# Retention's products as sums of two-part products, short tails stacked into full-height operands, key parts kept in the sample states' buffers

## The chip, the cores and the metric

The kernel runs on one core of a Trainium2 chip. The metric is the device time of one execution in microseconds (us), and lower is better. A core has a matrix engine (TensorE, PE in the profile, with its weight loads as PEld), a vector engine (VectorE, DVE), a scalar engine (ScalarE, ACT), GpSimd (POOL) and a queue engine (SyncE, SP) which here issues almost all DMA transfers.

## The reference

One layer of a decoder trunk for 256 prompt tokens, 16 learned meta tokens ahead of them, and 8 sample tokens, which makes T = 280 columns (TL = 264 without the meta tokens). All of it is in fp32.

```python
x <- LN1(alpha*x + 0.5*SwiGLU_1(x))      # 2048 -> 5504 -> 2048
x <- LN2(alpha*x + Mixer(x))             # x @ w_in (2048 -> 10*2048), retention + HGRN2, gates, w_out
x <- LN3(alpha*x + 0.5*SwiGLU_2(x))
```

The mixer has two branches. Retention has 8 heads with 256 key and 256 value features and a fixed decay per head: the outputs are (q k^T * D) v, normalised over the head's features by mean and variance, and the prompt's state is the sum over tokens of decayed k times v. HGRN2 has 16 heads of 128 features with a learned forget gate, and its prompt state is likewise a sum over tokens. The sample tokens each update a state of their own (`state_ret`, `state_hgrn`), which is read, updated, written back and multiplied with the sample's query.

## The kernel before

Activations lie with features on the 128 partitions and tokens along the free dimension, as 16 chunks of 128 features. Each dense product is made of parts: an fp32 operand is split into a rounded part `hi` (type fp32r, made by ScalarE) and a rest `lo` (made by VectorE), and a 128x128 block of weights takes three matmuls, whi*xhi, whi*xlo and wlo*xhi (`dense`, lines 196 to 198). Weights stream in units of 8 blocks: SP loads `raw`, ScalarE makes `whi` (L170), VectorE makes `wlo` (L171), with three buffers for each (`stream`). A matmul with plain fp32 operands appears in the profile as two instructions.

The order on TensorE is written out by hand; the other engines' instructions are put in order by the compiler's planner, by priority and by due times that it models. Engines and the SP queue work strictly in the order they were given.

In the mixer, the loop `for u in range(HR)` projects six groups of two output chunks (f, q_h, i_h, q_r, k_r, v_r) for head pair u and then four gate groups for u-1. A group walks over the 16 chunks of x, and after each chunk, that is after 6 dense matmuls, `pump()` counts one step for every running thread. A thread is a Python generator, `mix_hg` for two HGRN2 heads or `mix_ret` for one retention head; `yield n` means that its next piece of TensorE work is put in n steps later. `start(gen, 3)` starts a thread three steps after the group that completes its inputs. `evacuate` for the gates of u needs the threads of u to be done.

`mix_ret` does, in order: transposes of v (L780) and k (L786) through a PSUM bank, decayed keys `kt` (L788), scores `psc` (L799) and their decay (`mul(scr...)`, with the table `dtab`), the prompt state `psr` (L811) for two halves c, the sample states in two halves e (loads L825, scaling on ScalarE L826, update on VectorE L829, store L832, product `pqr` L838), the outputs `por` (L852, and L854 for the samples), the mean `pm` (L861) and the variance. `mix_hg` transposes v (L637), makes the within-chunk attention over seven levels, and then for each of its two heads h transposes the keys (L717), copies them out (`kth` L718, and the 16 meta rows `ktm` L719), updates the sample states (L726, L727), and after `yield 6` makes the state products `pst` (L735 with the 16-row operands, L736, L737).

The tokens are 16 + 256: as blocks of 128 rows they leave a 16-row tail (the last tokens in `mix_ret`, the meta tokens in `mix_hg`), so that one matmul of each state sum and each output has operands 16 rows high.

`tmp(name, ...)` gives a buffer: either one of its own in the pool `mp` or, for the names in `rows`, one of the row tiles d0 to d15, ls1 and so on, which other names use at other times. `smr` has three buffers, for the retention sample states. `y` (the mixer's output in parts) has hi and lo of chunk c apart by 288 values for c below `Y_SPACED` and by 264 from there on.

Of the kernel before, what the change touches and what calls it, by code (L numbers as in the profile page):

```python
# [18 lines left out]
P = 128  # L19
# [4 lines left out]
NMETA, SEQ, NS = 16, 256, 8  # L24
LP = NMETA + SEQ
T = LP + NS
TL = T - NMETA
# [6 lines left out]

WT = U * P + 64
XT = 576
Y_SPACED = 12
XL = {T: 296, T + 2: 284, TL: 288, TL + 2: 288}
HL = {T: 296, TL: 288}
SG = {T: 296, TL: TL}  # L40
# [12 lines left out]
SCORES = ((0, 0, SEQ, P), (SEQ, P - NMETA, 2 * P - P + NMETA, P), (2 * SEQ - P + NMETA, SEQ - NMETA, NMETA, LP - 2 * P))  # L53
NSC = SCORES[2][0] + SCORES[2][2]
# [58 lines left out]
def trunk(ctx: ExitStack, tc: tile.TileContext, A, O):  # L113
    nc = tc.nc
    cst = ctx.enter_context(tc.tile_pool(name="cst", bufs=1))
# [24 lines left out]
    olb = cst.tile([P, KC], F32, tag="olb", name="olb")  # L140
    dec = cst.tile([P, 3, HR], F32, tag="dec", name="dec")
    sel = cst.tile([P, NS], F32, tag="sel", name="sel")
    msk = cst.tile([P, MASKED + 1, 2 * P], U8, tag="msk", name="msk")
    lnb = cst.tile([P, 2, 2, KC], F32R, tag="lnb", name="lnb")
    nc.vector.memset(ones, 1.0)
# [56 lines left out]
    def split(hi, lo, x):  # L202
        nc.scalar.copy(hi, x)
        nc.vector.tensor_tensor(out=lo, in0=x, in1=hi.bitcast(F32), op=ALU.subtract)

    def sums(out, hilo, part=slice(None)):

        for i, x in enumerate(hilo):
            nc.tensor.matmul(out, ones_r, x[:, part], start=i == 0, stop=i == 1)

    def mul(out, a, b):
        nc.vector.tensor_tensor(out=out, in0=a, in1=b, op=ALU.mult)

    def add(out, a, b):
        nc.vector.tensor_tensor(out=out, in0=a, in1=b, op=ALU.add)
# [253 lines left out]
    nc.sync.dma_start(ident, A["ident"])  # L469
    nc.sync.dma_start(dec, A["dec"])  # L470
    nc.sync.dma_start(sel, A["sel"])

    norm1 = ffn(1, up1, A["w_dn1"], 1)


    with tc.tile_pool(name="yp", bufs=1) as yp:
        yh, yl = [None] * KC, [None] * KC
        with tc.tile_pool(name="mp", bufs=1) as mp:

            rows = {n: (r if isinstance(r, list) else [r]) for n, r in {  # L480
# [3 lines left out]
            }.items()}  # L484
# [22 lines left out]
            st = {}  # L507
# [4 lines left out]
            qdr = tmp("qdr", (P, 2, NS * 32))  # L512
            nc.gpsimd.memset(qdh, 0.0)
            nc.gpsimd.memset(qdr, 0.0)
            threads = []

            def pump(_=None):
# [8 lines left out]
            def start(gen, wait):  # L526
                threads.append([gen, wait])
# [16 lines left out]
            def evacuate(n, c0, c1, o0, o1):  # L544
# [16 lines left out]
                elif n == "i_h":  # L561
                    v = tmp("v", (P, 2, T))
                    nc.scalar.copy(v[:, 0, :], o0)
                    nc.scalar.copy(v[:, 1, :], o1)
                    start(mix_hg(c0 // 2, st["f"], st["k"], st["q"], v), 3)
                elif n in ("q_r", "k_r"):
                    sc, w, x0 = (1.0, TL, NMETA) if n == "q_r" else (KSC, T, 0)
                    r = tmp(n, (P, 2, w))
# [36 lines left out]
            NB2 = LP - 2 * P  # L605
            BLOCKS = ((0, P), (P, P), (2 * P, T - 2 * P))

            def rows_out(src, width, tag):

                scr = drp.tile([NS, width], F32, tag=tag + "d", name=tag + "d")  # L610
                nc.sync.dma_start(scr, src)
                return scr

            def mix_hg(u, f, k, q, v):
# [9 lines left out]
                for i in range(3):  # L624
# [6 lines left out]
                vt = tmp("vth", (P, 2, 4, P))  # L631
                vrow = []
                for h in range(2):

                    pt = mx_bank("pt")
                    for b, (t0, n) in enumerate(((NMETA, P), (NMETA + P, P), (0, NMETA), (T - NMETA, NMETA))):
                        nc.tensor.transpose(pt[:n, b * P : (b + 1) * P], v[:, h, t0 : t0 + n], ident)  # L637
                    nc.scalar.copy(vt[:, h, 0:2, :], pt[:, : 2 * P].rearrange("p (b f) -> p b f", b=2))
                    nc.scalar.copy(vt[:NMETA, h, 2:4, :], pt[:NMETA, 2 * P :].rearrange("p (b f) -> p b f", b=2))
                    vrow.append(rows_out(vt[8:16, h, 3, :], P, f"vh{h}"))  # L640
                    yield 1
                yield 5
                pd = mx_bank("pd")
# [67 lines left out]
                on_h[u] = on  # L711
                for h in range(2):
                    kt = tmp("kth", (P, 2, P))
                    ktm = tmp("ktm", (P, P))
# [4 lines left out]
                    nc.scalar.copy(ktm[:NMETA, :], pt[:NMETA, 2 * P : 3 * P])  # L719

                    vb = tmp("vbh", (P, NS, P))
                    nc.sync.dma_start(vb, vrow[h].partition_broadcast(P))
# [5 lines left out]
                            out=sm[:, b, :], in0=vb[:, b, :], scalar=k[:, h, LP + b : LP + b + 1], in1=sm[:, b, :],  # L728
                            op0=ALU.mult, op1=ALU.add)
                    nc.sync.dma_start(O["sgs"][2 * u + h], sm)  # L730
                    yield 6

                    S = tmp("Sh", (P, 3, P))
                    pst = mx_bank("pst")
                    nc.tensor.matmul(pst[:, 0:P], ktm[:NMETA, :], vt[:NMETA, h, 2, :], start=True, stop=True)  # L735
                    nc.tensor.matmul(pst[:, P : 2 * P], kt[:, 0, :], vt[:, h, 0, :], start=True, stop=True)  # L736
                    nc.tensor.matmul(pst[:, 2 * P : 3 * P], kt[:, 1, :], vt[:, h, 1, :], start=True, stop=True)  # L737
                    nc.scalar.copy(S[:, 0, :], pst[:, :P])
# [31 lines left out]
                done_h.add(u)  # L770

            def mix_ret(u, q, k, v):
                vt = tmp("vtr", (P, 3, 2, P))
                kt = tmp("ktr", (P, 3, 2, P))
                dt = tmp("dtab", (P, NSC))
                nc.sync.dma_start(dt, A["dtab"][u])
                for c in range(2):
                    pt = mx_bank("pt")
                    for b, (t0, n) in enumerate(BLOCKS):
                        nc.tensor.transpose(pt[:n, b * P : (b + 1) * P], v[:, c, t0 : t0 + n], ident)  # L780
                    nc.scalar.copy(vt[:, 0:2, c, :], pt[:, : 2 * P].rearrange("p (b f) -> p b f", b=2))
                    nc.scalar.copy(vt[: BLOCKS[2][1], 2, c, :], pt[: BLOCKS[2][1], 2 * P : 3 * P])
                    yield 1
                    pt = mx_bank("pt")
                    for b, (t0, n) in enumerate(BLOCKS):
                        nc.tensor.transpose(pt[:n, b * P : (b + 1) * P], k[:, c, t0 : t0 + n], ident)  # L786
                    for b, (t0, n) in enumerate(BLOCKS):
                        nc.vector.tensor_scalar(  # L788
                            out=kt[:n, b, c, :], in0=pt[:n, b * P : (b + 1) * P], scalar1=dec[:n, b, u : u + 1],
                            scalar2=None, op0=ALU.mult)  # L790
                    yield 2
                nc.vector.tensor_copy(qdr[:, :, 0 : NS * 32 : 33], q[:, :, SEQ:])
                vtf = vt.rearrange("p b c f -> p b (c f)")
                vrow = rows_out(vtf[16:24, 2, :], 256, "vr")
# [7 lines left out]
                scr = dt  # L802
                c2 = SCORES[2][0]
                mul(scr[:, :c2], psc[:, :c2], dt[:, :c2])
                mul(scr[:NB2, c2:], psc[:NB2, c2:NSC], dt[:NB2, c2:])
                yield 2

                for c in range(2):
                    pst = mx_bank("psr")
                    for b, nr in enumerate((P, P, NB2)):  # L810
                        nc.tensor.matmul(pst[:, :256], kt[:nr, b, c, :], vtf[:nr, b, :], start=b == 0, stop=b == 2)  # L811
                    so = tmp("sro", (P, 256))
                    nc.scalar.copy(so, pst[:, :256])
                    nc.sync.dma_start(O["srp"][u, c], so)
                    yield 2

                os = tmp("osr", (P, 256))
                for e in range(2):
# [23 lines left out]
                        nc.scalar.copy(os, pq[:, :256])  # L842
                    else:
                        add(os, os, pq[:, :256])
                yield 3

                on = tmp("on_r", (P, 2, TL), bufs=2)
                on_r[u] = on
                for c in range(2):
                    po = mx_bank("por")  # L850
                    for b, (col, l0, n, nk) in enumerate(SCORES):
                        nc.tensor.matmul(  # L852
                            po[:, l0 : l0 + n], vt[:nk, b, c, :], scr[:nk, col : col + n], start=b == 0, stop=b == 2)
                    nc.tensor.matmul(po[:, SEQ:TL], os[:, c * P : (c + 1) * P], sel, start=True, stop=True)  # L854
                    nc.scalar.copy(on[:, c, :], po[:, :TL])
                    yield 1
                sm_ = tmp("sqr", (P, TL))
                add(sm_, on[:, 0, :], on[:, 1, :])
                yield 6
                pm = mx_bank("pm")  # L860
                nc.tensor.matmul(pm[:, :TL], ones, sm_, start=True, stop=True)  # L861
# [147 lines left out]
```

## Time and profile before

| | |
|---|---|
| three timed runs | 2843.91, 2850.09, 2852.86 us; median 2850.09 us |
| the profiled execution | 2834.7 us, its span 2832.9 us |
| granted TensorE clock | 0.998 |
| PE busy, VectorE busy, ScalarE busy | 2806.4 us, 1687.5 us, 1329.4 us |
| moved by DMA | 536.27 MB, mean 189 GB/s |

The span is the time from the first to the last instruction of the profiled execution. PE's busy time counts matmuls that overlap in the pipeline, so the occupation of the engine by one matmul is read from the distance of its start to the next one's start, not from its duration.

### The profile page before, as it was taken

What the parts mean: (1) busy time and instruction counts of PE and PEld (TensorE: products, weight loads), DVE (VectorE), ACT (ScalarE), POOL (GpSimd) and SP (SyncE); (2) the same over time, 40 slices, a digit from 0 to 9 for tenths busy, and PEclk for the clock granted to TensorE, in tenths of its full rate; (3) what the DMA queues carried; (4) which work ended last, traced back from release to release, by engine and by line L of the source; (5) the groups of instructions that cost most, each with busy time, mean ns of one, the idle gap of its engine ahead of it and who ended that gap; (6) DMA issues with size and microseconds to landing.
All of it is one profiled execution on the core that took longest, in us unless ns stands there. A gap on an engine that the chain in (4) does not pass through costs nothing.

```text
span 2832.9 us, 54281 instructions
## 1 busy us (share of the span) xinstructions
PE 2806.4 (99%) x22704; PEld 2753.0 (97%) x22704; DVE 1687.5 (60%) x2677; ACT 1329.4 (47%) x1931; POOL 3.4 (0%) x38
## 2 busy tenths in 40 slices
PE   9999999999999999999999999999999999999999
PEld 9999999999989999999999999989999999999998
DVE  5444444555586766676767676766884444446444
ACT  4444443443364564646464555545554444444333
POOL 0000000000000000000000000000000000000000
PEclk9999999999999999999999999999999999999999
DMA  6555555555556565656565666655555555555554
GB/s 223 173 176 173 172 175 175 171 173 175 174 186 215 197 229 191 226 193 226 197 222 198 223 195 222 195 195 178 179 179 179 183 182 179 181 183 180 179 180 141
DMA packets 154438, 536.27 MB, mean 189 GB/s; under 512 B 17808, under 2 KB 25936, under 8 KB 154192
## 3 DMA queue, kind: packets, MB, share of 16 engines
q1 hardware_dynamic: 154048, 532.65, 57.7%
q8 instruction: 178, 2.92, 0.4%
q14 instruction: 68, 0.56, 0.1%
q10 hardware_dynamic: 144, 0.14, 0.0%
HBM read 502.12 MB, written 30.61 MB: 188 GB/s over the span
## 4 chain that ended last, share of the span: by engine, by line
PE 95%; ACT 2%; DMA 1%; DVE 1%; issue 0%; SPq 0%; ACTq 0%; DVEq 0%
PE up L197 12%; PE up L198 12%; PE up L196 12%; PE dn L197 6%; PE dn L198 6%; PE dn L196 6%; PE pj_g_r L196 1%; PE pj_v_r L196 1%; PE pj_k_r L196 1%; PE pj_k_r L197 1%; PE pj_v_r L197 1%; PE pj_k_r L198 1%; PE pj_v_r L198 1%; PE pj_g_h L196 1%; PE wo L196 1%; PE wo L197 1%
## 5 line engine op out<-in xcount | busy, mean ns | idle before, releaser
L171 DVE TENSOR_TENSOR wlo<-raw,whi 128x1024 fp32r<-128x1024 f32 (+1 forms) x869 | 1062.8, 1223 | 900.6 <-ACT whi L170 897.1
L170 ACT CAST whi<-raw 128x1024 fp32r<-128x1024 f32 (+1 forms) x869 | 909.9, 1047 | 1137.2 <-PE up L197 481.2
L198 PE MATMUL up<-x,wlo 128*128 128x280 f32 (+1 forms) x2688 | 774.8, 288 | 1.2 <-DVE wlo L171 1.2
L197 PE MATMUL up<-x,whi 128*128 128x280 f32 (+1 forms) x2688 | 773.6, 288 | 0.0
L196 PE MATMUL up<-x,whi 128*128 128x280 f32 (+1 forms) x2688 | 765.8, 285 | 1.4 <-ACT whi L170 1.4
L196 PEld LDWEIGHTS up<-x,whi 128*128 128x128 f32 x2688 | 506.8, 189 | 2.0 <-ACT whi L170 2.0
L198 PEld LDWEIGHTS up<-x,wlo 128*128 128x128 f32 x2688 | 505.2, 188 | 1.8 <-DVE wlo L171 1.7
L197 PEld LDWEIGHTS up<-x,whi 128*128 128x128 f32 x2688 | 505.3, 188 | 0.0
L198 PE MATMUL dn<-h,wlo 128*128 128x280 f32 (+1 forms) x1376 | 396.1, 288 | 0.0
L197 PE MATMUL dn<-h,whi 128*128 128x280 f32 (+1 forms) x1376 | 395.6, 288 | 0.0
L196 PE MATMUL dn<-h,whi 128*128 128x280 f32 (+1 forms) x1376 | 391.9, 285 | 0.0
L196 PEld LDWEIGHTS dn<-h,whi 128*128 128x128 f32 x1376 | 259.1, 188 | 0.1
L197 PEld LDWEIGHTS dn<-h,whi 128*128 128x128 f32 x1376 | 258.4, 188 | 0.1
L198 PEld LDWEIGHTS dn<-h,wlo 128*128 128x128 f32 x1376 | 258.2, 188 | 0.0
L196 PE MATMUL pj_g_r<-x,whi 128*128 128x264 f32 x256 | 81.4, 318 | 0.0
L197 PE MATMUL pj_i_h<-x,whi 128*128 128x280 f32 x256 | 74.9, 292 | 2.7 <-DVE x L364 2.7
L196 PE MATMUL pj_g_h<-x,whi 128*128 128x264 f32 x256 | 76.8, 300 | 0.0
L196 PE MATMUL pj_i_h<-x,whi 128*128 128x280 f32 x256 | 74.2, 290 | 1.4 <-ACT f L549 0.7
L196 PE MATMUL pj_v_r<-x,whi 128*128 128x280 f32 x256 | 75.1, 293 | 0.0
L196 PE MATMUL pj_k_r<-x,whi 128*128 128x280 f32 x256 | 75.1, 293 | 0.0
L197 PE MATMUL pj_k_r<-x,whi 128*128 128x280 f32 x256 | 74.5, 291 | 0.0
L197 PE MATMUL pj_v_r<-x,whi 128*128 128x280 f32 x256 | 74.5, 291 | 0.0
(337 smaller groups left out, 5151.9 us busy)
## 6 DMA issues: line engine op xcount, KB each, us to landing
raw<-in_w_up SPq DMA_DIRECT2D x343, 512.0 KB, 3.6
raw<-in_w_in SPq DMA_DIRECT2D x320, 512.0 KB, 3.6
raw<-in_w_dn SPq DMA_DIRECT2D x172, 512.0 KB, 3.5
smr<-in_sr SPq DMA_DIRECT2D x32, 512.0 KB, 5.9
out_srs<-smr SPq DMA_DIRECT2D x32, 512.0 KB, 3.7
raw<-in_w_out SPq DMA_DIRECT2D x32, 512.0 KB, 3.6
smh<-in_sg SPq DMA_DIRECT2D x16, 512.0 KB, 4.0
out_sgs<-smh SPq DMA_DIRECT2D x16, 512.0 KB, 6.1
```

The source lines that it names most:

```text
L170: nc.scalar.copy(hi[:, j0:j1, :], raw[:, j0:j1, :])
L171: nc.vector.tensor_tensor(out=lo[:, j0:j1, :], in0=raw[:, j0:j1, :], in1=hi[:, j0:j1, :].bitcast(F32), op=ALU.subtract)
L196: nc.tensor.matmul(o, wh, h, start=k == 0, stop=False)
L197: nc.tensor.matmul(o, wh, l, start=False, stop=False)
L198: nc.tensor.matmul(o, wl, h, start=False, stop=k == nk - 1)
```

## The change

It concerns the mixer's threads, the buffers they use, and one constant.

- In `mix_ret`, v, the decayed keys, the decayed scores, the sample outputs `os` and the sum under the mean are split into hi and lo parts, and `psr`, `por`, the sample columns and `pm` are made of fp32r products: three for an operand pair of which both are split, two for a split operand with an exact one (`sel_r`, `ones_r`).
- `stack` writes a 16-row operand into a 128-row tile that is zero elsewhere, hi at two of the rows 0, 32 and 64 and lo at the third. One operand has lo at 32 and the other at 64, so that one fp32r matmul over 128 rows gives the three part products. Five `stack` calls per retention head (v and k of two halves, the scores) and four per HGRN2 thread (v and k of two heads) use it. The tiles are zeroed once, at the mixer's start.
- The key parts are tiles of the tag `smr`, so the three sample buffers also hold the keys; `dtab` comes in two pieces in the row tiles of `rot`; the tail of v lies in the row tile of `osr`, the tail of k in that of `sro`.
- Waits in steps: `yield 6` becomes 9 ahead of `pst`, `yield 3` becomes 5 ahead of `por`; the second HGRN2 thread (u = 1) starts after 25 steps and not after 3.
- `Y_SPACED` goes from 12 to 0.

The diff below is cut. Left out are: the scores, which are decayed in two pieces (256 and 144 columns) that are each split into `sch` and `scl`, with their 16-row tail stacked into `ss3`; and `por`, which has three products for each of two blocks, one for the tail (`vs3` with `ss3`) and two for the sample columns (`orh` and `orl` with `sel_r`).

```diff
-Y_SPACED = 12
+Y_SPACED = 0
+PARTS = (0, 32, 64)
...
     sel = cst.tile([P, NS], F32, tag="sel", name="sel")
+    sel_r = cst.tile([P, NS], F32R, tag="sel_r", name="sel_r")
...
+            vs3, ks3 = tmp("vs3", (P, 2, P), dt=F32R), tmp("ks3", (P, 2, P), dt=F32R)
+            ss3 = tmp("ss3", (P, NMETA), dt=F32R)
+            vm3, km3 = tmp("vm3", (P, 2, P), dt=F32R), tmp("km3", (P, P), dt=F32R)
+            for t in (vs3[:, 0, :], vs3[:, 1, :], ks3[:, 0, :], ks3[:, 1, :], vm3[:, 0, :], vm3[:, 1, :], km3, ss3):
+                nc.scalar.copy(t, qdh[:, 0, : t.shape[-1]])
+            def stack(tile_of, src, lo_at):
+                hi_at = [at for at in PARTS if at != lo_at]
+                first, other, low = (tile_of(slice(at, at + NMETA)) for at in hi_at + [lo_at])
+                nc.scalar.copy(first, src)
+                nc.scalar.copy(other, src)
+                nc.vector.tensor_tensor(out=low, in0=src, in1=first.bitcast(F32), op=ALU.subtract)
...
-                    start(mix_hg(c0 // 2, st["f"], st["k"], st["q"], v), 3)
+                    start(mix_hg(c0 // 2, st["f"], st["k"], st["q"], v), 25 if c0 == 2 else 3)
...
-                    nc.scalar.copy(vt[:NMETA, h, 2:4, :], pt[:NMETA, 2 * P :].rearrange("p (b f) -> p b f", b=2))
+                    nc.scalar.copy(vt[:NMETA, h, 2, :], pt[:NMETA, 3 * P :])
+                    stack(lambda r: vm3[r, h, :], pt[:NMETA, 2 * P : 3 * P], 32)
...
-                    nc.scalar.copy(ktm[:NMETA, :], pt[:NMETA, 2 * P : 3 * P])
+                    stack(lambda r: km3[r, :], pt[:NMETA, 2 * P : 3 * P], 64)
...
-                    yield 6
+                    yield 9
-                    nc.tensor.matmul(pst[:, 0:P], ktm[:NMETA, :], vt[:NMETA, h, 2, :], start=True, stop=True)
+                    nc.tensor.matmul(pst[:, 0:P], km3, vm3[:, h, :], start=True, stop=True)
...
-                vt = tmp("vtr", (P, 3, 2, P))
-                kt = tmp("ktr", (P, 3, 2, P))
-                dt = tmp("dtab", (P, NSC))
+                vh, vl = tmp("vtr", (P, 2, 2, 2, P), dt=F32R).rearrange("p e b c f -> e p b c f")
+                kh, kl = tmp("ktr", (P, 2, 2, 2, P), dt=F32R, bufs=3, tag="smr").rearrange("p e b c f -> e p b c f")
+                vtl = tmp("vtl", (P, 2, P))
+                dts = [tmp("dtab", (P, SEQ)), tmp("dtab", (P, NSC - SEQ))]
...
+                    split(vh[:, :, c, :], vl[:, :, c, :], pt[:, : 2 * P].rearrange("p (b f) -> p b f", b=2))
+                    nc.scalar.copy(vtl[: BLOCKS[2][1], c, :], pt[: BLOCKS[2][1], 2 * P : 3 * P])
+                    stack(lambda r: vs3[r, c, :], vtl[:NB2, c, :], 32)
...
+                    for b in range(2):
+                        nc.vector.tensor_scalar(out=kh[:, b, c, :], in0=kb, scalar1=d, scalar2=None, op0=ALU.mult)
+                        nc.vector.scalar_tensor_tensor(
+                            out=kl[:, b, c, :], in0=kb, scalar=d, in1=kh[:, b, c, :].bitcast(F32), op0=ALU.mult, op1=ALU.subtract)
+                    ktl = tmp("sro", (P, P))
+                    nc.scalar.activation(ktl[:NB2, :], pt[:NB2, 2 * P : 3 * P], AF.Copy, scale=dec[:NB2, 2, u : u + 1])
+                    stack(lambda r: ks3[r, c, :], ktl[:NB2, :], 64)
...
-                    for b, nr in enumerate((P, P, NB2)):
-                        nc.tensor.matmul(pst[:, :256], kt[:nr, b, c, :], vtf[:nr, b, :], start=b == 0, stop=b == 2)
+                    for b in range(2):
+                        for i, (a, x) in enumerate(((kh, vh), (kh, vl), (kl, vh))):
+                            nc.tensor.matmul(
+                                pst[:, :256], a[:, b, c, :], x[:, b].rearrange("p c f -> p (c f)"), start=b + i == 0, stop=False)
+                    nc.tensor.matmul(pst[:, :256], ks3[:, c, :], vs3.rearrange("p c f -> p (c f)"), start=False, stop=True)
...
-                yield 3
+                hilo = tmp("orh", (P, 256), dt=F32R), tmp("orl", (P, 256), dt=F32R)
+                split(*hilo, os)
+                yield 5
...
+                hilo = tmp("rhi", (P, TL), dt=F32R), tmp("rlo", (P, TL), dt=F32R)
+                split(*hilo, sm_)
                 yield 6
-                nc.tensor.matmul(pm[:, :TL], ones, sm_, start=True, stop=True)
+                sums(pm[:, :TL], hilo)
```

More of the change, by code (lines that the diff above doesn't have):

```diff
@@ L471, in trunk @@
     nc.sync.dma_start(sel, A["sel"])
+    nc.scalar.copy(sel_r, sel)
     norm1 = ffn(1, up1, A["w_dn1"], 1)
@@ L630, in mix_hg @@
                     split(hilo[0][:, i], hilo[1][:, i], pr)
-                vt = tmp("vth", (P, 2, 4, P))
+                vt = tmp("vth", (P, 2, 3, P))
                 vrow = []
@@ L638, in mix_hg @@
                     nc.scalar.copy(vt[:, h, 0:2, :], pt[:, : 2 * P].rearrange("p (b f) -> p b f", b=2))
-                    nc.scalar.copy(vt[:NMETA, h, 2:4, :], pt[:NMETA, 2 * P :].rearrange("p (b f) -> p b f", b=2))
-                    vrow.append(rows_out(vt[8:16, h, 3, :], P, f"vh{h}"))
+                    nc.scalar.copy(vt[:NMETA, h, 2, :], pt[:NMETA, 3 * P :])
+                    stack(lambda r: vm3[r, h, :], pt[:NMETA, 2 * P : 3 * P], 32)
+                    vrow.append(rows_out(vt[8:16, h, 2, :], P, f"vh{h}"))
                     yield 1
@@ L713, in mix_hg @@
                     kt = tmp("kth", (P, 2, P))
-                    ktm = tmp("ktm", (P, P))
                     pt = mx_bank("ptk")
@@ L772, in mix_ret @@
             def mix_ret(u, q, k, v):
-                vt = tmp("vtr", (P, 3, 2, P))
-                kt = tmp("ktr", (P, 3, 2, P))
-                dt = tmp("dtab", (P, NSC))
-                nc.sync.dma_start(dt, A["dtab"][u])
+                vh, vl = tmp("vtr", (P, 2, 2, 2, P), dt=F32R).rearrange("p e b c f -> e p b c f")
+                kh, kl = tmp("ktr", (P, 2, 2, 2, P), dt=F32R, bufs=3, tag="smr").rearrange("p e b c f -> e p b c f")
+                vtl = tmp("vtl", (P, 2, P))
+                dts = [tmp("dtab", (P, SEQ)), tmp("dtab", (P, NSC - SEQ))]
+                for d, at in zip(dts, (0, SEQ)):
+                    nc.sync.dma_start(d, A["dtab"][u, :, at : at + d.shape[1]])
                 for c in range(2):
@@ L780, in mix_ret @@
                         nc.tensor.transpose(pt[:n, b * P : (b + 1) * P], v[:, c, t0 : t0 + n], ident)
-                    nc.scalar.copy(vt[:, 0:2, c, :], pt[:, : 2 * P].rearrange("p (b f) -> p b f", b=2))
-                    nc.scalar.copy(vt[: BLOCKS[2][1], 2, c, :], pt[: BLOCKS[2][1], 2 * P : 3 * P])
+                    split(vh[:, :, c, :], vl[:, :, c, :], pt[:, : 2 * P].rearrange("p (b f) -> p b f", b=2))
+                    nc.scalar.copy(vtl[: BLOCKS[2][1], c, :], pt[: BLOCKS[2][1], 2 * P : 3 * P])
+                    stack(lambda r: vs3[r, c, :], vtl[:NB2, c, :], 32)
                     yield 1
@@ L786, in mix_ret @@
                         nc.tensor.transpose(pt[:n, b * P : (b + 1) * P], k[:, c, t0 : t0 + n], ident)
[L787 to L790, printed above, removed]
+                    for b in range(2):
+                        kb, d = pt[:, b * P : (b + 1) * P], dec[:, b, u : u + 1]
+                        nc.vector.tensor_scalar(out=kh[:, b, c, :], in0=kb, scalar1=d, scalar2=None, op0=ALU.mult)
[4 more added lines that the diff above has]
+                    stack(lambda r: ks3[r, c, :], ktl[:NB2, :], 64)
                     yield 2
                 nc.vector.tensor_copy(qdr[:, :, 0 : NS * 32 : 33], q[:, :, SEQ:])
-                vtf = vt.rearrange("p b c f -> p b (c f)")
-                vrow = rows_out(vtf[16:24, 2, :], 256, "vr")
+                vrow = rows_out(vtl[16:24].rearrange("p c f -> p (c f)"), 256, "vr")
                 psc = mx_bank("psc")
@@ L801, in mix_ret @@
                             start=c == 0, stop=c == 1)
-                scr = dt
                 c2 = SCORES[2][0]
-                mul(scr[:, :c2], psc[:, :c2], dt[:, :c2])
-                mul(scr[:NB2, c2:], psc[:NB2, c2:NSC], dt[:NB2, c2:])
+                sch = tmp("sch", (P, c2), dt=F32R)
+                scl = tmp("scl", (P, c2), dt=F32R)
+                for d, at, n in zip(dts, (0, SEQ), (SEQ, c2 - SEQ)):
+                    mul(d[:, :n], psc[:, at : at + n], d[:, :n])
+                    split(sch[:, at : at + n], scl[:, at : at + n], d[:, :n])
+                tail = dts[1][:NB2, c2 - SEQ :]
+                mul(tail, psc[:NB2, c2:NSC], tail)
+                stack(lambda r: ss3[r, :], tail, 64)
                 yield 2
@@ L850, in mix_ret @@
                     po = mx_bank("por")
[L851 to L854, printed above, removed]
+                    for b, (col, l0, n, _) in enumerate(SCORES[:2]):
+                        for i, (x, w) in enumerate(((vh, sch), (vl, sch), (vh, scl))):
+                            nc.tensor.matmul(
+                                po[:, l0 : l0 + n], x[:, b, c, :], w[:, col : col + n], start=b + i == 0, stop=False)
+                    l0 = SCORES[2][1]
+                    nc.tensor.matmul(po[:, l0 : l0 + NMETA], vs3[:, c, :], ss3, start=False, stop=True)
+                    for i, x in enumerate(hilo):
+                        nc.tensor.matmul(po[:, SEQ:TL], x[:, c * P : (c + 1) * P], sel_r, start=i == 0, stop=i == 1)
                     nc.scalar.copy(on[:, c, :], po[:, :TL])
```

2 rows, old and new, of the table rows are left out of this document.

## Prediction

> **What bounds the kernel now.** I read the page's totals first, then the chain that ended last, then stretches of the mixer, then TensorE's rows in order of time.
>
> ```profile
> span 2832.9 us, 54281 instructions
> PE 2806.4 (99%) x22704; PEld 2753.0 (97%) x22704; DVE 1687.5 (60%) x2677; ACT 1329.4 (47%) x1931; POOL 3.4 (0%) x38
> PE 95%; ACT 2%; DMA 1%; DVE 1%; issue 0%; SPq 0%; ACTq 0%; DVEq 0%
> L171 DVE TENSOR_TENSOR wlo<-raw,whi 128x1024 fp32r<-128x1024 f32 (+1 forms) x869 | 1062.8, 1223 | 900.6 <-ACT whi L170 897.1
> 1145.00:1290.00 145.00, 143.81 (x1187) 138.09 (x1186) 98.47 (x181) 77.75 (x129) 0.00 (x0) 1.00 0.62 208
> ```
>
> TensorE is never short of work: 95% of the chain is its own. The last row is one pass of the mixer (145 us for one head pair; its columns are PE, PEld, DVE, ACT, POOL, clock, DMA share): VectorE works 68% of it, ScalarE 54%. So the time moves by what TensorE is spared in the 8 passes, and by waits that go or come. The profiled execution took 2834.7 us, the median run 2850.09, which is 15.4 more; I sum against the profiled one and carry the difference over unchanged.
>
> **The change part by part.** Prices are distances between starts of successive rows. First the state products of both branches:
>
> ```profile
> 1140.79 1.65 PE L811 MATMUL psr<-vtr,ktr 128*128 128x256 f32 x6
> 1142.37 0.39 PE L196 MATMUL pj_g_r<-x,whi 128*128 128x264 f32 x1
> 1142.60 0.29 PE L197 MATMUL pj_g_r<-x,whi 128*128 128x264 f32 x1
> ...
> 1143.08 0.28 PE L198 MATMUL pj_a_r<-x,wlo 128*128 128x264 f32 x1
> 1143.29 0.48 PE L735 MATMUL pst<-vth,ktm 16*128 16x128 f32 x2
> 1143.71 0.49 PE L736 MATMUL pst<-vth,kth 128*128 128x128 f32 x2
> ...
> 1144.17 0.37 PE L196 MATMUL pj_g_r<-x,whi 128*128 128x264 f32 x1
> 1144.38 0.28 PE L197 MATMUL pj_g_r<-x,whi 128*128 128x264 f32 x1
> ```
>
> A dense product is 0.12 apart from the next. The first one behind a group still shows the group's tail, so a group costs the start of the second one behind it, less 0.12, less its own start. Hence `psr` costs 1142.60 - 0.12 - 1140.79 = 1.69 us and `pst` 1144.38 - 0.12 - (1143.08 + 0.12) = 1.06 us. Outputs and mean:
>
> ```profile
> 1174.81 1.16 PE L852 MATMUL por<-dtab,vtr 128*128 128x256 f32 x6
> 1175.90 0.39 PE L854 MATMUL por<-sel,osr 128*128 128x8 f32 x2
> ...
> 1176.35 0.29 PE L197 MATMUL pj_g_r<-x,whi 128*128 128x264 f32 x1
> ...
> 1184.20 0.61 PE L861 MATMUL pm<-sqr,ones 128*128 128x264 f32 x2
> ...
> 1184.77 0.28 PE L197 MATMUL pj_g_h<-x,whi 128*128 128x264 f32 x1
> ```
>
> `por` costs 1.42 us, `pm` 0.45. What products of parts cost is seen in the HGRN2 levels, which have them already, and the price of a narrow matmul in the fp32 ones:
>
> ```profile
> 1095.96 0.28 PE L209 MATMUL pl<-prodsmh,ones_r 128*128 128x256 f32 x1
> 1096.08 0.28 PE L209 MATMUL pl<-prodvbh,ones_r 128*128 128x256 f32 x1
> ...
> 1107.09 1.00 PE L669 MATMUL pl<-Q,K 128*128 128x64 f32 x8
> ...
> 1108.11 0.29 PE L197 MATMUL pj_k_r<-x,whi 128*128 128x280 f32 x1
> ```
>
> A product of parts with 256 columns takes 0.12. Eight fp32 instructions of 64 columns take 1108.11 - 0.12 - 1107.09 = 0.90, or 0.11 each, although they move a quarter of the columns: a floor, which I ascribe to the weight load. No product of parts narrower than 256 is in the trace; its bounds are this 0.11 and its share of columns (144/256 of 0.12 = 0.07, next to nothing for 8 or 16). I take 0.11, since it is the nearest row with a full weight load and few columns.
>
> - `psr`, 16 times: seven products at 0.12 = 0.84; spared 0.85 each, 13.6 us.
> - `por`, 16 times: three of 256 columns (0.36) and six narrow ones (three of 144, the tail, two sample ones) at 0.11 (0.67) = 1.03; spared 0.39 each, 6.2 us. By share of columns 0.59, spared 13.3 us.
> - `pst`, 16 times: the meta product becomes one of parts, with the four fp32 instructions of L736 and L737 five at 0.11 = 0.56; spared 0.50 each, 8.0 us (8.8 with the first at 0.06).
> - `pm`, 8 times: 0.24 for 0.45; 1.7 us.
>
> Sum 29.5 us, up to 37.4. The Trainium skill, "TensorE: Matmul & The Clock Gate", section Back-to-back issue gap, gives a sustained 81 ns per matmul at 128 columns, faster than the 0.11 I use. By it `por` would come to 0.85 and spare 9.1 us, and the sum would be near 32.5; no row here shows a narrow product of parts, so this stays an estimate beside mine.
>
> **Waits that go.** TensorE's list of waits, and the chain in the pass around 1170:
>
> ```profile
> PE pst L735 <- ACT ktm L719: 9.3, 8, 2.1
> PE pd L209 <- ACT prodsmh L203: 3.9, 2, 2.0
> ...
> 1158.82 0.61 PE pqr L838 x8
> ...
> 1159.45 5.70 DMA smr<-in_sr
> ...
> 1168.18 0.42 ACT rr L226
> 1168.61 0.93 ACT whi L170
> 1169.54 0.17 ACT ktm L719
> ...
> 1169.75 0.48 PE pst L735 x2
> ```
>
> One `pst` per pass waits 1.2 us on average, because ScalarE, strictly in order, has sat behind a sample state's load that the previous sample product released. `yield 9` puts `pst` 3 steps of 6 products later, 3 x 0.72 = 2.2 us. But the stacked tail needs a copy and then a VectorE subtraction, some 0.3 to 1 us more, depending on what is queued there. Ends: all 9.3 gone, or nothing gained. I take 6.5, since 2.2 less 0.6 covers all but the longest wait and scraps. The second entry is the start of the first two HGRN2 threads, 2.0 us each; the second one competes for `smh` and `vbh` with the first thread's last head, and 22 steps later that thread has ended: 2.0 gained (0 to 2.0). Together 8.5 (0 to 11.3).
>
> **What is added.** The small work per pass, by these rows:
>
> ```profile
> L782 ACT COPY vtr<-pt 24x128 f32<-24x128 f32 x16 | 4.0, 250 | 0.0
> L788 DVE TENSOR_SCALAR ktr<-pt,dec 128x128 f32<-128x128 f32 x32 | 9.8, 347 | 23.6 <-PE pt L786 23.6
> L788 DVE TENSOR_SCALAR ktr<-pt,dec 24x128 f32<-24x128 f32 x16 | 5.3, 331 | 0.0
> L204 DVE TENSOR_TENSOR prodvbh<-pr,prodsmh 128x256 fp32r<-128x256 f32 x40 | 15.4, 417 | 0.0
> ```
>
> VectorE: nine stack subtractions (9 x 0.33), four key rests (4 x 0.35), six rests of splits and one more decay (7 x 0.42), less two tail scalings: 6.6 us, so 98 becomes 105 of about 141 us. ScalarE: 18 stack copies less 2 removed, 2 scalings (18 x 0.25) and four casts at about 0.4: 6 us, so 78 becomes 84. Both still idle a quarter of the pass or more. That hides the work; it isn't free where a TensorE group stands soon behind it. `psr` comes 3.6 us after the last decayed key now (1137.2 to 1140.79); the rest of the keys and the stacked tail need about 2 of that. `por` has two more steps (1.4 us) for the 0.8 us of its split, `pm` six steps as before for 0.85 us. I charge 2 us in all; the ends are 0 and, at 1 us for two groups of each pass, 16.
>
> The second transfer of `dtab` is one more issue per pass on SP; it now waits for `rot` and no longer for `por`, and it is needed only at the scores, 25 steps on: nothing. The keys in `smr` are a matter of when loads start:
>
> ```profile
> 1130.00:1135.00 5.00, 5.00 (x45) 4.93 (x44) 3.13 (x6) 1.96 (x6) 0.00 (x0) 1.00 0.50 156
> 1145.00:1180.00 35.00, 33.81 (x287) 30.51 (x286) 23.27 (x46) 21.60 (x39) 0.00 (x0) 1.00 0.90 297
> ```
>
> Three of a pass's four state loads now come early, one in this crowded stretch (0.90 of the DMA). Later the third one too has to wait, for the second `psr`. 512 KB more at 297 GB/s is 1.8 us of transfer, hidden by the weights made ahead (three buffers of 24 products, 2.9 us each); nothing in the forecast.
>
> The mixer's start gets eight zeroing copies and `sel_r` on ScalarE (9 x 0.25 = 2.2 us) while LN1 is applied, and the first thread's stacks: 1 us (0 to 3). `Y_SPACED`:
>
> ```profile
> 2012.84 0.28 PE L196 MATMUL wo<-y,whi 128*128 128x264 f32 x1
> ...
> 2014.28 0.28 PE L196 MATMUL wo<-y,whi 128*128 128x264 f32 x1
> ...
> 2015.74 0.28 PE L196 MATMUL wo<-y,whi 128*128 128x264 f32 x1
> ```
>
> These are starts of chunks 8, 12 and 0 of the next group: four spaced chunks take 1.44 us, the four unspaced ones 1.46. So 12 chunks more cost 0.06 us in each of 16 outputs, 1.0 us.
>
> Sum: -29.5 - 8.5 + 2 + 1 + 1 = -34.0 us. The profiled execution would come to 2800.7 us, the median to **2816.1 us**.
>
> **The rivals.**
>
> *More than forecast*: narrow products go by their columns and all the waits go, -37.4 - 11.3 + 2 = -46.7: 2803 us. For it: the floor of 0.11 comes from fp32 instructions, which may load weights slower than parts do. Chance 0.17.
>
> *The waits stay*: the planner puts the stacks behind weight splits on VectorE (1.2 us each, L171 above) and `pst` still waits, -29.5 + 4 and 0 to 8 of new waits: 2825 to 2833. For it: ScalarE's crowded stretch, in which one copy of 0.25 us came 1.2 us late. Chance 0.18.
>
> *No change*: the longer queues on both engines stop TensorE 3 to 4 us more per pass, at `psr`, `pst` and `por`; 2845 to 2855. Against it: both engines idle 27% and more. Chance 0.07.
>
> *Slower, by the sample buffer*: SP works in order. If the load into the keys' buffer is queued ahead of weights and waits there for the second `psr`, weights stop behind it. TensorE notices once that lasts longer than the weights' lead (at most two buffers of 24 products, 5.8 us; I take 4), and it decides from 4 + 4.3 us per pass on (34/8 = 4.3); at 10 us 2816 + 8 x 6 = 2864. For it: the buffer is released late. Against it: the loads of this kernel are put in order by when their buffers come free. Chance 0.04.
>
> *Slower, by addresses*: `sel_r` stands ahead of activations and weights and moves them all by 32 bytes. The 20,856 dense products (869 x 24) would need 1.7 ns each to eat the gain; at 3 ns it is 2879. For it: the chunks above differ by place. Against it: operands and weights move together, and those differ in distance. Chance 0.04.
>
> **How the numbers follow.** The forecast has 0.50. 0.3% (8.6 us) is about what a measurement tells from no change: faster 0.50 + 0.17 + 0.18 = 0.85, same 0.07, slower 0.08. The range takes in the better case and the waits that stay, 2800 to 2838, and leaves the last three cases out.
>
> **What would show it.** In the profile after: `psr` 0.84 and `por` about 1.0 from start to start; no 16-row matmul; the list's first wait at 3 us or less; VectorE near 105 us per pass; dense products 0.12 apart as before. The prediction is wrong if `por` or `pst` stays above 1 us by new waits, if weights (`whi`, `wlo`) turn up as releasers in the mixer, or if dense products moved by a nanosecond or more.

## The result and the profile after

| kernel | median, us (lowest to highest; runs) | ratio to the kernel before, 95% interval |
|---|---|---|
| before, in the same set | 2843.91 (2836.39 to 2852.86; 5) | |
| changed | 2830.58 (2828.60 to 2832.84; 5) | 0.9948 (0.9925 to 0.9972) |

The change makes the kernel 13.3 us faster by the medians; 34.0 were forecast. The two profiled executions lie only 4.1 us apart (2834.7 and 2830.58): before's profile fell 9.2 us under its median, the changed kernel's on it. The stages are therefore compared between the profiles, and those explain 4.1 us; where the other 9.2 us lie, no profile shows.

The totals and the chain of the page of the changed kernel:

```profile
span 2828.6 us, 54706 instructions
...
PE 2794.1 (99%) x22720; PEld 2759.8 (98%) x22720; DVE 1723.7 (61%) x2821; ACT 1370.5 (48%) x2114; POOL 3.4 (0%) x38
...
PE 93%; DVE 2%; DMA 2%; ACT 1%; issue 1%; SPq 0%; ACTq 0%; DVEq 0%
```

TensorE's share of the chain fell from 95% to 93%: the work went down, and waits came in. The stretches of mixer, output weights and second up stage, first of before, then of the changed kernel (columns: length, then PE, PEld, DVE, ACT, POOL busy, granted clock, DMA share, GB/s):

```profile
794.50:1968.40 1173.90, 1156.35 (x9478) 1107.11 (x9477) 808.48 (x1511) 631.28 (x1057) 2.18 (x14) 1.00 0.62 206
1968.40:2061.90 93.50, 93.37 (x772) 93.03 (x771) 74.74 (x159) 46.34 (x67) 0.40 (x4) 1.00 0.57 181
2061.90:2564.70 502.80, 502.80 (x4135) 502.67 (x4134) 266.41 (x325) 221.46 (x284) 0.00 (x0) 1.00 0.56 181
```

```profile
795.00:1969.30 1174.30, 1148.49 (x9494) 1118.52 (x9493) 844.90 (x1655) 672.44 (x1239) 2.18 (x14) 0.98 0.63 206
1969.30:2063.70 94.40, 94.27 (x772) 93.93 (x771) 74.72 (x159) 46.35 (x67) 0.40 (x4) 1.00 0.55 179
2063.70:2560.70 497.00, 497.00 (x4135) 496.87 (x4134) 266.44 (x325) 221.63 (x284) 0.00 (x0) 1.00 0.58 183
...
1176.00:1182.80 6.80, 6.80 (x33) 6.80 (x33) 1.12 (x3) 2.69 (x5) 0.00 (x0) 0.50 0.45 140
```

The mixer, where almost the whole change lies, takes 1174.3 us for 1173.9: it gained nothing. The gain that the profile shows is the 5.8 us of the second up stage, whose code the change doesn't touch. The mixer's mean clock fell to 0.98; the last row shows where: stretches at half clock. There are eight of them in the mixer, 47.8 us together; before had one of 3.4.

TensorE's list of waits:

```profile
PE por L889 <- ACT orh L205: 8.4, 6, 1.9
PE pj_i_h L198 <- DVE q L214: 6.2, 1, 6.2
PE por L889 <- DVE orl L206: 4.6, 6, 0.8
PE pd L211 <- ACT prodsmh L205: 2.0, 1, 2.0
```

`pst` is gone from the list; `por` stands in its place, 13.0 us in pairs at 6 places, and there is one new wait of 6.2 us. All waits in the mixer went from 17.3 to 25.6 us. The products themselves, in TensorE's rows:

```profile
1140.23 0.88 PE L838 MATMUL psr<-vtr,ktr 128*128 128x256 f32 x6
...
1141.07 0.28 PE L198 MATMUL pj_g_r<-x,whi 128*128 128x264 f32 x1
...
1144.80 0.22 PE L750 MATMUL pst<-vm,km 128*128 128x128 f32 x1
...
1145.47 0.28 PE L199 MATMUL pj_g_r<-x,whi 128*128 128x264 f32 x1
```

`psr` costs 0.84 us and `pst` 1145.47 - 0.12 - 1144.80 = 0.55, as forecast. `pm` measures 0.24. `por` has waits inside here; without them it takes 1.02 to 1.09, mostly 1.03 (below, third set of runs). So the products spare 16 x 0.85 + 16 x 0.51 + 16 x 0.37 + 8 x 0.21 = 29.4 us, against 29.5 forecast. The mixer's balance is then -29.4 + 8.3 (waits) + C = +0.4. C = 21.5 us is a remainder, not a measurement: it holds the half clock, which half of 47.8, less half of 3.4, bounds at 22.2, and the small work added at the mixer's start.

### The profile page after: what moved, and what is told of

The parts are those of the page before. It is cut to its first block, busy times and chain, and to the rows that moved or that the text cites. A ratio compares the mean times of both kernels' runs of the same rounds, so it can differ in the third digit from the quotient of the medians.

```text
span 2828.6 us, 54706 instructions
## 1 busy us (share of the span) xinstructions
PE 2794.1 (99%) x22720; PEld 2759.8 (98%) x22720; DVE 1723.7 (61%) x2821; ACT 1370.5 (48%) x2114; POOL 3.4 (0%) x38
## 4 chain that ended last, share of the span: by engine, by line
PE 93%; DVE 2%; DMA 2%; ACT 1%; issue 1%; SPq 0%; ACTq 0%; DVEq 0%
PE up L199 12%; PE up L198 12%; PE up L200 12%; PE dn L199 6%; PE dn L200 6%; PE dn L198 6%; DMA smr<-in_sr 2%; PE pj_v_r L198 1%; PE pj_f L199 1%; PE pj_k_r L198 1%; PE pj_k_r L199 1%; PE pj_v_r L199 1%; PE pj_f L198 1%; PE pj_f L200 1%; PE pj_k_r L200 1%; PE pj_v_r L200 1%
## 5 line engine op out<-in xcount | busy, mean ns | idle before, releaser
L200 PE MATMUL up<-x,wlo 128*128 128x280 f32 (+1 forms) x2688 | 764.7, 284 | 1.2 <-DVE wlo L173 1.2
L858 DVE SCALAR_TENSOR_TENSOR smr<-vbr,k_r,smr 128x256 f32<-128x256 f32 x128 | 55.2, 479 | 39.1 <-DMA vbr<-vrd 38.2
L200 PE MATMUL pj_i_h<-x,wlo 128*128 128x280 f32 x256 | 75.7, 296 | 0.0
L198 PE MATMUL pj_k_r<-x,whi 128*128 128x280 f32 x256 | 75.1, 293 | 0.0
L198 PE MATMUL pj_v_r<-x,whi 128*128 128x280 f32 x256 | 75.1, 293 | 0.0
```

The source lines that it names most:

```text
L198: nc.tensor.matmul(o, wh, h, start=k == 0, stop=False)
L200: nc.tensor.matmul(o, wl, h, start=False, stop=k == nk - 1)
L858: nc.vector.scalar_tensor_tensor(out=sm[:, j, :], in0=vb[:, j, :], scalar=k[:, c, t : t + 1], in1=sm[:, j, :], op0=ALU.mult, op1=ALU.add)
```

## The experiments

All are made from the changed kernel unless said otherwise. Each kernel of the first two sets was run once, so its time is read together with the stages and waits of its profile. The first set looks at the two new waits.

What makes `por` late is read on VectorE of the changed kernel:

```profile
1159.86 0.88 DVE L858 SCALAR_TENSOR_TENSOR smr<-vbr,k_r,smr 128x256 f32<-128x256 f32 x2 [5.63 <-DMA vbr<-vrd]
...
1171.28 1.22 DVE L173 TENSOR_TENSOR wlo<-raw,whi 128x1024 fp32r<-128x1024 f32 x1
1172.42 1.39 DVE L742 SCALAR_TENSOR_TENSOR smh<-vbh,k,smh 128x128 f32<-128x128 f32 x5
1173.73 0.41 DVE L217 TENSOR_TENSOR osr<-osr,pqr 128x256 f32<-128x256 f32 x1
...
1175.20 0.41 DVE L206 TENSOR_TENSOR orl<-osr,orh 128x256 fp32r<-128x256 f32 x1
```

and on TensorE at the same time:

```profile
1172.55 0.22 PE L887 MATMUL por<-ss,vs 128*128 128x16 f32 x1
1174.63 0.27 PE L889 MATMUL por<-sel_r,orh 128*128 128x8 f32 x1 [1.86 <-ACT orh L205]
1175.66 0.27 PE L889 MATMUL por<-sel_r,orl 128*128 128x8 f32 x1 [0.76 <-DVE orl L206]
```

The sample columns could start at 1172.6. The addition that makes `osr` ends at 1174.1, because a weight split and the updates of the second HGRN2 head's `smh` stand ahead of it in VectorE's order. In the kernel before, those eight updates ran between 1159.9 and 1164.3. The first row shows a second cause of lateness: VectorE stands 5.63 us for the load of the sample's v rows (`vbr`) and then has no pause until `osr`. Such waits come to 38.2 us in the changed kernel and to 26.1 before. e5 below has only 25.1 of them and `por` waits all the same, so they are not needed for it; what share they have in the changed kernel's 13.0 us is not shown.

**e1_por_later**: more distance ahead of `por`.

```diff
-                yield 5
+                yield 9
```

> The changed kernel with yield 9 for yield 5 ahead of por (four more steps, 2.9 us; the waits at por are 1.5 to 2.6 us). Theory A (the products are as cheap as forecast, and what they spare is lost at one place: por waits for osr and its split, 13.0 us in six passes, and TensorE's clock is halved for 6.8 us after each of five of these waits): waits before por under 1 us, the half-clock windows at 1176, 1323, 1470, 1756 and 1903 us gone, the span 24 to 30 us shorter than 2828.6, near 2802. Rival B (the stretch is bound by the sample states' loads and by VectorE, so a wait that is taken from por turns up at the next group, pm, pv or the next pass): span above 2820 and other waits of 8 us or more.

Measured: 2804.96 us, span 2802.9. The mixer's stretch and what is left of the wait:

```profile
795.70:1943.60 1147.90, 1133.35 (x9495) 1102.94 (x9494) 846.11 (x1655) 670.16 (x1239) 2.17 (x14) 0.99 0.64 211
```

```profile
PE pj_i_h L198 <- DVE q L214: 5.5, 1, 5.5
...
PE por L889 <- DVE orl L206: 0.4, 1, 0.4
```

13.0 us of waits at `por` became 0.4, half clock fell from 47.8 to 13.7 us, and the mixer lost 26.4. So 12.6 us of waiting had cost about 26. The second half is the clock: 34.1 us less at half clock are worth up to 17.1, and no half-clock stretch is left behind any `por`.

**e2_first_thread_6**: the first thread alone without the new step, for the wait of 6.2 us near 916.

```diff
-                    yield 9
+                    yield 9 if u else 6
```

> The changed kernel with yield 6 instead of 9 ahead of pst in the first thread (u = 0) alone. Theory A (three steps later means the second head's state update holds f of the first pair when f of the second is to be written, so i_h waits 6.2 us at 916 us and the clock is halved for 6.8 us): that wait falls to about 1 us, as in the kernel before (0.7), the window at 920 us goes, span 6 to 9 us shorter, near 2821. Rival C (the wait comes from ScalarE and VectorE standing behind late loads of v rows and retention states, which this doesn't touch): the wait stays at 5 us or more, span 2827 to 2830.

Measured: 2837.64 us, mixer 1179.0.

```profile
PE pj_i_h L198 <- ACT f L564: 7.3, 1, 7.3
```

The wait is still there and lasts 7.3, so it doesn't need the longer distance ahead of `pst`. The kernel took longer than either theory had it.

**e4_os_not_split**: the sample columns of `por` as fp32 products again, no split of `os`.

```diff
-                hilo = tmp("orh", (P, 256), dt=F32R), tmp("orl", (P, 256), dt=F32R)
-                split(*hilo, os)
...
-                    for i, x in enumerate(hilo):
-                        nc.tensor.matmul(po[:, SEQ:TL], x[:, c * P : (c + 1) * P], sel_r, start=i == 0, stop=i == 1)
+                    nc.tensor.matmul(po[:, SEQ:TL], os[:, c * P : (c + 1) * P], sel, start=True, stop=True)
```

> The changed kernel with the sample outputs os left in fp32 (one fp32 matmul with sel in place of orh and orl with sel_r), yield 5 kept: the split ahead of por undone. Theory A (osr itself is late on VectorE, behind state updates that came late): por still waits in most passes, 13.0 us become 5 to 9, some half-clock windows stay, span 2812 to 2824. Rival D (the split's two further steps are the wait): por waits under 2 us in all, no half-clock window behind por, span near 2803.

Measured: 2815.67 us, mixer 1157.1.

```profile
PE por L886 <- DVE osr L217: 5.8, 6, 1.9
```

`por` still waits at the same 6 places, now for `osr` itself: about 5.8 of the 13.0 us are the late sum, and the rest goes with the split's two operations behind it. Half clock follows the longest two of these waits, 1.9 and 1.5 us, and none of the shorter ones (0.9 us and less).

**e5_steps_alone**: the kernel before, with only the two changed waits in steps of the HGRN2 threads.

```diff
-                    start(mix_hg(c0 // 2, st["f"], st["k"], st["q"], v), 3)
+                    start(mix_hg(c0 // 2, st["f"], st["k"], st["q"], v), 25 if c0 == 2 else 3)
...
-                    yield 6
+                    yield 9
```

> The kernel before with the changed steps alone (yield 9 ahead of pst, the second HGRN2 thread at 25), fp32 products and buffers as before. Theory A: the waits at pst (9.3 us) and at the second thread's start (2.0) go, and the wait of i_h for f near 916 us grows from 0.7 to 5 or 6 us with a half-clock window behind it; span 2822 to 2830 against 2832.9. Rival C (the long i_h wait needs the keys in the sample buffers): i_h waits about 1 us, span 2820 to 2823.

Measured: 2855.04 us, mixer 1193.9, which is 20.0 worse than before instead of better. Its waits, and VectorE at the first of them:

```profile
PE por L854 <- DVE osr L215: 11.7, 6, 2.3
PE pj_i_h L196 <- DVE q L212: 5.3, 1, 5.3
PE pvr L209 <- DVE rlo L204: 5.2, 7, 1.0
```

```profile
1179.85 1.22 DVE L171 TENSOR_TENSOR wlo<-raw,whi 128x1024 fp32r<-128x1024 f32 x1
1180.98 0.61 DVE L727 SCALAR_TENSOR_TENSOR smh<-vbh,k,smh 128x128 f32<-128x128 f32 x2
1181.51 0.41 DVE L215 TENSOR_TENSOR osr<-osr,pqr 128x256 f32<-128x256 f32 x1
```

The `pst` wait is gone, and the same chain as in the changed kernel (split, `smh`, `osr`) now holds up `por`. None of the new products, splits or key buffers is in this kernel. So the steps alone move the wait from `pst` to `por`, and the wait near 916 comes with them too.

The second set undoes single steps.

**e6_pst_at_6**: all products, the old distance ahead of `pst`.

```diff
-                    yield 9
+                    yield 6
```

> The changed kernel with yield 6 ahead of pst in all threads, all else as changed. Theory A2 (after the steps alone gave 11.7 us of waits at por: three more steps in the first head put the second head's eight state updates ahead of osr on VectorE, so the wait moves from pst to por): waits before por at most 3 us, waits before pst 8 to 14 us, at most two half-clock windows behind them, span 2805 to 2815. Rival B2 (por waits because the cheaper products bring TensorE to it sooner): por still waits 8 us or more and the windows stay, span 2825 or above.

Measured: 2858.92 us, mixer 1202.7.

```profile
PE pst L750 <- DVE km L529: 22.7, 6, 4.2
PE pvr L211 <- ACT rhi L205: 16.4, 8, 3.2
PE pj_i_h L198 <- ACT f L564: 8.6, 1, 8.6
```

The `por` waits vanish, but `pst` waits for its stacked tail, 3.8 us each and 22.7 in all, where 8 to 14 were expected, and the span of 2856.9 us is far above both theories. This is no clean proof for the theory: around 1180 VectorE still has the eight `smh` updates (1181.5 to 1183.7) ahead of `osr` (1185.7), and `por` finds its sum ready after TensorE has stood at `pst`. What shows that the steps move the wait is e5. The changed kernel needs both: the 9 steps ahead of `pst`, which the stacks use up, and more than 5 ahead of `por`.

**e7_por_later_start_3**: e1_por_later, with the second HGRN2 thread at its old start. `vm3` and `km3` exist once, and with this start the second thread writes them while the first one still needs them, so the meta part of the states changes; its time is read for the wait alone.

```diff
-                    start(mix_hg(c0 // 2, st["f"], st["k"], st["q"], v), 25 if c0 == 2 else 3)
+                    start(mix_hg(c0 // 2, st["f"], st["k"], st["q"], v), 3)
...
-                yield 5
+                yield 9
```

> The changed kernel with yield 9 ahead of por and the second HGRN2 thread started after 3 steps again. Theory A3 (the 25 steps let the planner put the second pair's q and f behind late retention states, since nobody is due to use them; every run with 25 has this wait, 5.3 to 7.3 us): i_h waits 1 us or less near 916 us, no half-clock window there, the start of the second thread waits 2 us again; span 2794 to 2799. Rival C2 (the wait comes from the later loads and the two added steps): i_h waits 5 us or more, span 2802 to 2806.

Measured: 2806.90 us, mixer 1150.2; the wait for `q` near 916 is 5.6 us for 5.5. The wait doesn't need the late start, which is worth about 2 us here. At the second thread's start the 2.0 us of `pd` don't come back with the old start either; 3.5 us at `po` and 1.0 at `pl` near it do.

**e8_sel_r_alone** and **e9_y_spaced_0**: the kernel before, with only the new constant tile, or only the constant, to see which of them moved the second up stage.

```diff
+    sel_r = cst.tile([P, NS], F32R, tag="sel_r", name="sel_r")
...
+    nc.scalar.copy(sel_r, sel)
```

> The kernel before with the tile sel_r added (32 bytes per partition ahead of activations and weights) and filled by one copy, and nothing else. The second FFN's up products take 364.4 ns per weight block before and 360.0 after the change, 5.9 us in that stage. Theory E (the shifted addresses do it): that stage 497.0 us instead of 502.9, the others within 0.5 us, span near 2827. Rival F (Y_SPACED does it): the stage stays at 502.9, span 2832 to 2834.

```diff
-Y_SPACED = 12
+Y_SPACED = 0
```

> The kernel before with Y_SPACED = 0 alone. Theory E: w_out's stage 94.3 us instead of 93.4, the second FFN's up stage stays at 502.9, span near 2834. Rival F: w_out's stage 94.3 and the up stage 497.0, span near 2828.

Measured: 2830.18 and 2834.36 us. The second up stage of the first, then that of the second:

```profile
2063.50:2560.40 496.90, 496.90 (x4136) 496.76 (x4135) 266.36 (x325) 221.82 (x284) 0.00 (x0) 1.00 0.58 183
```

```profile
2070.40:2567.40 497.00, 497.00 (x4135) 496.87 (x4134) 266.44 (x325) 221.60 (x284) 0.00 (x0) 1.00 0.57 183
```

Either edit alone takes the whole 5.8 us away (502.8 before), each in one profiled execution. So neither theory holds as I had put it: it is no sum of two effects and no property of `sel_r`, but a switch that more than one edit throws. The stage of the output weights, 93.5 us before, takes longer with either edit too; in e8, where `Y_SPACED` stayed 12:

```profile
1969.20:2063.50 94.30, 94.16 (x771) 93.82 (x770) 74.74 (x159) 46.28 (x67) 0.40 (x4) 1.00 0.58 179
```

The third set takes the wait near 916 away and times the main kernels. ScalarE of the changed kernel there:

```profile
918.38 1.06 ACT L855 ACTIVATE smr<-smr 128x1024 f32<-128x1024 f32 x1 [3.92 <-DMA smr<-in_sr]
919.35 1.03 ACT L172 CAST whi<-raw 128x1024 fp32r<-128x1024 f32 x1
920.28 0.66 ACT L573 ACTIVATE q<-pj_q_h 128x264 f32<-128x264 f32 x2
...
923.30 0.70 ACT L564 ACTIVATE f<-pj_f 128x280 f32<-128x280 f32 x2
```

The decay of a sample state stands ahead of `q` and `f` on ScalarE and waits 3.9 us for its load.

**e10_first_ret_later**: e1_por_later, and the first retention thread starts 16 steps later, so that its sample states come behind `q` and `f`.

```diff
-                    start(mix_ret(c0 // 2, st["q_r"], st["k_r"], v), 3)
+                    start(mix_ret(c0 // 2, st["q_r"], st["k_r"], v), 19 if c0 == 0 else 3)
...
-                yield 5
+                yield 9
```

> The changed kernel with yield 9 ahead of por and, besides, the first retention thread (u = 0) started after 19 steps and not 3. Theory C (the wait of i_h near 916 us, 5.3 to 8.6 us in every run with new steps or new products, is ScalarE standing in its queue before a late retention state, with q and f of the second pair behind it): with these states 16 steps later the wait falls to 2 us or less, the half-clock window there goes, span 2793 to 2798, 5 to 9 us less than with yield 9 alone (2802.9). Rival H (the wait is for the HGRN2 states themselves, which hold f): it stays at 4 us or more, span 2800 to 2806.

**e11_por_later_timed** is e1_por_later and **e12_changed_timed** the changed kernel, on the same chip.

> The changed kernel with yield 9 ahead of por again, timed. Theory A: 2803 to 2808 us, a ratio to the kernel before of 0.984 to 0.989, since the waits that start half-clock windows are gone in every execution and not in the profiled one alone. Rival: windows come and go between executions, the times scatter by 10 us or more and their median is above 2812.

> The changed kernel itself, timed beside the other two on the same chip. Theory A: 2828 to 2833 us, 24 to 28 us over yield 9 alone, with the half-clock windows behind por in its profile again.

| kernel | median, us (lowest to highest; runs) | ratio to the kernel before, 95% interval |
|---|---|---|
| before | 2838.34 (2833.82 to 2854.15; 13) | |
| changed (e12) | 2829.25 (2825.19 to 2831.82; 10) | 0.9957 (0.9941 to 0.9974) |
| `por` later (e11) | 2802.98 (2800.76 to 2806.43; 4) | 0.9873 (0.9835 to 0.9910) |
| and first retention later (e10) | 2792.26 (2790.43 to 2794.79; 4) | 0.9831 (0.9800 to 0.9863) |

The four steps ahead of `por` are worth 26.3 us timed, the later first retention thread 10.7 more (5 to 9 were expected). The profile of e10, its mixer, ScalarE near 916 and one `por`:

```profile
PE 96%; DVE 1%; DMA 1%; ACT 1%; issue 0%; SPq 0%; ACTq 0%; DVEq 0%
```

```profile
798.20:1933.40 1135.20, 1126.87 (x9495) 1097.92 (x9494) 845.82 (x1655) 669.43 (x1239) 2.17 (x14) 1.00 0.65 213
```

```profile
916.09 0.70 ACT L564 ACTIVATE f<-pj_f 128x280 f32<-128x280 f32 x2
...
923.26 1.06 ACT L855 ACTIVATE smr<-smr 128x1024 f32<-128x1024 f32 x1
```

```profile
1168.49 0.40 PE L884 MATMUL por<-sch,vtr 128*128 128x256 f32 x2
...
1169.69 0.28 PE L199 MATMUL pj_g_h<-x,whi 128*128 128x264 f32 x1
```

`f` comes at 916.1 and the sample state after it; the wait is gone, and so is every half-clock stretch of the mixer. This `por` takes 1169.69 - 0.12 - 1168.49 = 1.08 us. The mixer is 38.7 us shorter than before, and the terms nearly add up: 29.4 of products, 17.3 - 7.9 = 9.4 of waits and up to 1.7 for before's one stretch at half clock make 40.5; the 1.8 us between may be the work added at the mixer's start, which no run takes out. This version beats both kernels.

## Why the prediction was right or wrong

The sign and the range held, the sum did not (2830.58 us for 2816.1): the mixer was to lose 29.5 + 8.5 - 2 - 1 = 35.0 us and, in the profiles, lost none.

- *Products*: right, 29.4 for 29.5. `psr` and `pst` are on the forecast to 0.01 us, and `por` at about 1.03 is the floor's value, not that by columns (0.59). The first rival falls with this. That the floor comes out so exactly is partly luck: single narrow products are 0.06 to 0.11 apart, and `por` reaches 1.03 with the 0.08 us by which the dense products behind it come late.
- *Waits that go*: `pst` lost all 9.3 us (6.5 taken) and `pd` the 2.0 forecast. That three more steps cover the wait at `pst` was right, but e5 shows that it is half an account: the wait that left `pst` stands at `por`. The reason given for `pd` is not shown, since its wait stayed away in e7 as well.
- *What is added*: this is the step that failed. The prediction charged 2 us "in all" for new waits and said of `por` that it had "two more steps (1.4 us) for the 0.8 us of its split". It took the start of that split, the sum `osr`, as unmoved. With three steps more in the first HGRN2 head, the second head's `smh` updates stand on VectorE just ahead of it. `por` waited 13.0 us, inside the ends 0 to 16 but far from the value taken. What the moved steps do to the order on VectorE was not worked out. The amount of work was not at fault: VectorE got 4.6 us more per pass (6.6 forecast), ScalarE 5.1 (6).
- *The clock*: not in the prediction at all. About 21 us go here, more than the 13.0 us of waits at `por`. e1 and e10 show it by taking the waits away: 12.6 us of waits are worth 26.4. With the changed kernel's waits priced once, the mixer would have come to -29.4 + 8.3 = -21 us, and the half clock behind them takes that away again.
- *The rival "the waits stay"* comes nearest: its 2825 to 2833 holds the time, and new waits of 8.3 us are just beyond its 0 to 8. But its place was wrong (at `pst`; that is what e6 shows, where `pst` was not moved), and it reaches its time only together with the clock and the second up stage.
- *The start of the mixer*: `sel_r` and the zeroing, 1 us forecast, is not to be seen apart; the wait of 6.2 us near 916 was not foreseen. It comes from the order on ScalarE, where the decay of a sample state went ahead of `q` and `f`; e10 shows it. e2 and e7 show that the wait stays when either changed step is taken back, e5 that the two together suffice without the new products. Whether the products alone would make it was not tried, and why the order comes out so each time stays open.
- *Output weights*: 0.9 us for 1.0 forecast, but e8 shows 0.8 of it without the change of `Y_SPACED`, so the number came out and its reason is not shown. *Addresses*: dense products did move, and to the other side, 5.8 us less in one stage where the rival feared a loss.
- *Its own signs*: two of the three signs of being wrong came: `por` went above 1 us by new waits, and dense products moved by 1.4 ns in the second up stage. Weights did not turn up as releasers in the mixer.
- *Keys in the sample buffers*: no wait for weights appears in TensorE's list in the mixer, so the sample-buffer rival falls. "Nothing" is not shown: VectorE's waits for `vbr` grew from 26.1 to 38.2 us. With the keys and the old distance ahead of `pst` (e6) they are 26.8, with the new steps and no keys (e5) 25.1, so the growth needs both the step and something of the new products or buffers. Keys in buffers of their own were not tried, for lack of room.

## What to carry to other kernels

A wait taken away by moving a step is not gone until the engine behind it has been followed: list what the moved step now runs in front of on every in-order engine, and ask which TensorE group stands behind that. Count a TensorE stall of 1.5 us or more at about twice its length (26.4 us for 12.6 here), because the clock can halve behind it for several microseconds; in e5 it did so behind two of six such stalls, so this is a mean and no rule for one stall. After a change has been made, read the new list of waits before judging the idea: here four steps in one line were worth twice what the whole change had brought.

## What the runs showed of the hardware

**Short waits halve the clock.** In the changed kernel five of the six pairs of `por` waits, 1.8 to 2.6 us together, are each followed by 6.8 us at a clock of 0.50; the sixth, 0.73 and 0.76 us, is not. In e4 waits of 1.9 and 1.5 us did it, and shorter ones did not; in e5 only two of six waits of 1.7 to 2.3 us did. The stretches last 3.41 us or 2, 3 or 4 times that, and dense products of 264 columns come 0.22 us apart in them for 0.12. The Trainium skill, "TensorE: Matmul & The Clock Gate", Part 1, tells of a clock of 4/8 or 8/8, decided over free-running windows of about 3.4 us. The trace agrees with the 0.50 and the 3.41. It agrees with free-running windows too: all stretches of a run begin whole multiples of 3.413 us apart, in the changed kernel those at 848.33, 920.01 and 1176.01 by 4, 25 and 100 of them behind the one at 834.67. On this grid the window from 1172.59 to 1176.01 holds both waits of its pair, 2.62 us, and half clock follows. In e5 the two waits that did it lie with 1.65 and 1.79 us inside one window; of the other four no window holds more than 1.64, since borders cut them. So it matters where a wait falls, and the changed kernel run again (e12) has waits of the same kind but only 34.1 us at half clock in its mixer for 47.8. No sharp bound comes out: in e12 1.24 us of idle time in a window was followed by half clock, in e11 1.89 was not. The Trainium skill's advice on the same page, section "Why this matters for your kernels", to avoid idle gaps over about 3 us is too lenient for this kernel: less than 2 us sufficed.

**Dense products of 264 columns have two speeds.** In the second up stage they come every 121.6 ns on the mean in the kernel before and in e5 (502.8 us for 4135 products), and every 120.2 ns in all others (497.0 us); the stage runs wholly in one or the other, at a clock of 1.00. By groups the `wlo` products, first of before and then of the changed kernel (busy time, then mean ns of one):

```profile
L198 PE MATMUL up<-x,wlo 128*128 128x264 f32 x1312 | 374.8, 286 | 0.0
```

```profile
L200 PE MATMUL up<-x,wlo 128*128 128x264 f32 x1312 | 364.7, 278 | 0.0
```

A constant tile of 32 bytes or the spacing of the mixer's output buffer (e8, e9) is enough to switch it. The stages don't switch together: from the start of the second down stage to the end the kernel before takes 268.2 us, the changed one 267.9 and e9 265.1. What sets the speed stays open.

**Narrow products of parts** come 0.06 to 0.11 us apart, with few exceptions. **Products with 16-row operands** among 128-row ones cost more than their size says: in the kernel before, `psr`'s plain fp32 instructions with 16 rows come 0.30 to 0.32 us apart, those with 128 rows 0.215. Stacking brought `pst` from 1.06 to 0.55 us, but the stacked product is also one of parts and no longer plain fp32, and no run separates the two.
